# State products of a Mamba-2 mixer: C's high and low parts side by side, three matmuls made into two

## The chip, the cores and the metric

The kernel runs on one core of a Trainium2 chip. Its time is the device time of one launch in microseconds (us), the median of several runs; lower is better. The engines are named as in the profile: PE does matmuls (PEld is its weight load), DVE and ACT do elementwise work, POOL little here, and SP issues transfers. Each engine takes its instructions in the order of its own queue.

## What is computed

One decoder block over 512 tokens of width 1024, in float32: a token mixer, a cross-attention into 256 memory tokens and a SwiGLU feed-forward layer, each behind an RMSNorm. The mixer has a Mamba-2 part of 16 heads of width 64 in two groups, and a pooling part. The change lies in the Mamba-2 part, whose core is this (four chunks of 128 tokens, 128 states):

```python
cb = jnp.einsum("bclgn,bcsgn->bgcls", cc, bc)
y_diag = jnp.einsum("bghcls,bcsghp->bclghp", cb[:, :, None] * seg, xc)
states = jnp.einsum("bcsgn,bghcs,bcsghp->bcghpn", bc, decay_states, xc)
...
_, prev = lax.scan(step, init, (jnp.moveaxis(states, 1, 0), jnp.moveaxis(chunk_decay, -1, 0)))
y_off = jnp.einsum("bclgn,cbghpn,bghcl->bclghp", cc, prev, jnp.exp(a_cs))
```

`cc` is C, `bc` is B, `cb` the product of C with B in each chunk, and `y_off` what a chunk takes from the state left by the chunks before it.

## The kernel before

**Number format.** Every float32 operand of a matmul is split into a high part (a rounded copy, made by ACT) and a low part (the remainder, a subtraction on DVE). A product is three matmuls (`mm3`, L116 to L119): high by high, high by low, low by high, added up in PSUM. A name that ends in h or l is such a part, `whi` and `wlo` those of a weight. So `t_prh` and `t_prl` are the parts of a state, `t_cth` and `t_ctl` those of C.

**Slots.** The work is a table of slots (`SPEC`, L40 on). An item has up to three phases: prep ahead of its matmuls, its matmuls, and post behind them. The program is written slot by slot: post of the slot before and prep of the slot after, step by step in turn with the splitting of coming weights, then the slot's matmuls. A scheduler then makes the order of each engine's queue from this program by its own estimate of when operands are there, and gives out the buffers. Only the first slot keeps the written order.

**The items that matter here.**

- `cb:g` (L539): the product of C with B for group g, 12 matmuls of 128 columns into one PSUM bank. Its post multiplies by the causal mask on DVE (L552) into `t_cbm`.
- `s:g.c` (L586): the state left by chunk c, built up on DVE (L601, L603) as `t_prev`, then split (`t_prh` at L233 on ACT, `t_prl` at L241 on DVE).
- `P:j` (L624), one for each of eight pairs of heads (four pairs to a group). Its prep makes the decay matrix: eight relu on ACT (L645), exponentials (L651, L653), times `t_cbm` on DVE (L656), a high part `mh` on ACT (L660) and a low part `ml` on DVE (L663). Its matmuls are the state term `yo` (9 of 128 columns, three for each of chunks 1 to 3, which need the state left by chunks 0 to 2) and the diagonal product `pd` (12 of 256 columns). Its post makes `t_y` from `pd` (L687), multiplies `yo` by the decay E (L694) and adds it (L695).
- `v:m` and `p:g`: the pooling part's projection (24 matmuls of 512 columns) and its product `po` (12); post of `v` is a running sum on DVE (L749 to L754) and a split into `t_pdh`, `t_pdl`; post of `po` is a split into `t_pgh`, `t_pgl` (L235, L243). `z:m` is a gate's projection and `op:m` the pooling half of the output projection, 24 matmuls each.

The second group's part of the table is this; the place that the prediction speaks of is `P:4` and what lies around it:

```python
"v:4 t:1.2 s:1.0 g:3", "v:5 s:1.1", "p:1", "v:6 s:1.2", "P:4 v:7", "P:5 p:2", "z:7", "", "", "P:6 z:6 p:3",
"P:7", "op:0 g:5 op:1 op:2 g:6", ...
```

**Buffers.** PSUM has eight banks of 128x512 float32. Six of them are handed round to all products (`PS`, tag `ps`, L71); the other two are the single buffer of `pd`. A product's bank is free again when its post has read it.

Of the kernel before, what the change touches and what calls it, by code (L numbers as in the profile page):

```python
# [17 lines left out]
NC = 4  # L18
# [43 lines left out]
def hybrid_block(ctx: ExitStack, tc: tile.TileContext, a: dict, out: bass.AP,  # L62
                 act_bufs=69, la=1, wb=(6, 4, 5), eng="", dact=(0, 1), raw_n=6, warm=12, spec=None, start=START, smm=START_MM, hu=1, dbg=None):
    nc = tc.nc
# [27 lines left out]
    def col(i, rows=None):  # L92
        return vec[:, i:i + 1] if rows is None else vec[rows, i:i + 1]
# [22 lines left out]
    def mm3(ps, whi, wlo, xhi, xlo, start, stop):  # L116
        nc.tensor.matmul(ps, whi, xhi, start=start, stop=False)  # L117
        nc.tensor.matmul(ps, whi, xlo, start=False, stop=False)  # L118
        nc.tensor.matmul(ps, wlo, xhi, start=False, stop=stop)  # L119
# [103 lines left out]
    def need(*key):  # L223
        while key not in st:
            yield

    def splits(dsts, names, srcs, scale=None):

        out_ = []
        for (b, n), src in zip(names, srcs):  # L230
            hi = T(b + "h", F32R, n)
            if scale is None:
                nc.scalar.copy(hi, src)  # L233
            else:
                nc.scalar.activation(hi, src, AF.Identity, scale=scale)  # L235
            out_.append(hi)
        yield
        for key, (b, n), src, hi in zip(dsts, names, srcs, out_):
            lo = T(b + "l", F32R, n)
            if scale is None:  # L240
                nc.vector.tensor_tensor(out=lo, in0=src, in1=hi.bitcast(F32), op=ALU.subtract)  # L241
# [19 lines left out]
    st = {}  # L261
# [70 lines left out]
    def hold(it, name):  # L332
        it.ps = PS(name)
        return it.ps
# [157 lines left out]
    def i_xbc(i):  # L492
        m = XBC_ORDER[i]
        g = i // 6
        it = Item(keys=[("xbc", i)])

        def mm():
            proj(hold(it, "xbc"), ready[("xbc", i)], st["xg" if i < raw_n else "u"])

        def post():  # L500
            yield from need("r1")
            xr = mul("xr", it.ps, st["r1",]) if i < raw_n else it.ps
            y = T("cv")
            nc.scalar.activation(y, xr, AF.Identity, scale=col(V_CW + 3 * 12 + m), bias=col(V_CB + m))
            yield
            for s in (1, 2, 3):
                nc.vector.scalar_tensor_tensor(out=y[:, s:], in0=xr[:, :S - s],
                                               scalar=col(V_CW + (3 - s) * 12 + m),
                                               in1=y[:, s:], op0=ALU.mult, op1=ALU.add)
            nc.scalar.activation(y, y, AF.Silu)  # L510
            if i % 6 == 0:
                yield from splits([("B", g)], [("bt", 512)], [y])
                st["Bf", g] = y
            elif i % 6 == 1:
                yield from splits([("C", g)], [("ct", 512)], [y])
            else:
                st["xs", m] = y
            yield

        it.mm, it.post = mm, post  # L520
        return it


    def i_btm(g):
# [11 lines left out]
        it.mm, it.post = mm, post  # L536
        return it

    def i_cb(g):  # L539
        it = Item()  # L540

        def mm():
            bh, bl = st["B", g]
            ch, cl = st["C", g]
            ps = hold(it, "cb")
            for c in range(NC):
                cs = slice(c * P, (c + 1) * P)
                mm3(ps[:, cs], bh[:, cs], bl[:, cs], ch[:, cs], cl[:, cs], True, True)

        def post():  # L550
            t = T("cbm")
            nc.vector.tensor_tensor(out=t.rearrange("p (c l) -> p c l", l=P),  # L552
                                    in0=it.ps.rearrange("p (c l) -> p c l", l=P),
                                    in1=cmask.unsqueeze(1).broadcast_to([P, NC, P]), op=ALU.mult)
            st["cbm", g] = t

        it.mm, it.post = mm, post
        return it
# [65 lines left out]
    def i_pair(j, load=None):  # L624
        g, i = j // 4, j % 4
        it = Item()
        js = slice(i * P, (i + 1) * P)

        def prep():
            tok = st["tok"]  # L630
            if load is not None:
                load_abc(load)
            mh = act.tile([P, NC, 2, P], F32R, tag="m", name=nm("mh"), bufs=2)
            ml = act.tile([P, NC, 2, P], F32R, tag="m2", name=nm("ml"), bufs=2)
            E = st["E", j]
            Ds = []
            for q in range(2):
                h = 2 * j + q
                abc = st["abc", j][q]
                D = T("D")  # L640
                Ds.append(D)
                for c in range(NC):
                    cs = slice(c * P, (c + 1) * P)
                    if q in dact:
                        nc.scalar.activation(D[:, cs], abc[:, cs], AF.Relu, scale=-1.0,  # L645
                                             bias=tok[:, c, 32 + h:33 + h])
                    else:
                        nc.vector.tensor_scalar(out=D[:, cs], in0=abc[:, cs], scalar1=tok[:, c, 32 + h:33 + h],
                                                scalar2=0.0, op0=ALU.subtract, op1=ALU.min)
            yield  # L650
            nc.scalar.activation(E, E, AF.Exp)  # L651
            for q in range(2):
                nc.scalar.activation(Ds[q], Ds[q], AF.Exp, scale=-1.0 if q in dact else 1.0)  # L653
                yield
            for q in range(2):
                nc.vector.tensor_tensor(out=Ds[q], in0=Ds[q], in1=st["cbm", g], op=ALU.mult)  # L656
                yield
            Mv = [D.rearrange("p (c l) -> p c l", l=P) for D in Ds]
            for q in range(2):
                nc.scalar.copy(mh[:, :, q, :], Mv[q])  # L660
                yield
            for q in range(2):
                nc.vector.tensor_tensor(out=ml[:, :, q, :], in0=Mv[q], in1=mh.bitcast(F32)[:, :, q, :],  # L663
                                        op=ALU.subtract)
                yield
            it.mh, it.ml, it.E = mh, ml, E

        def mm():
            mh, ml = it.mh, it.ml
            ch, cl = st["C", g]  # L670
            it.po = PS("yo")
            for c in range(1, NC):
                ph, pl = st["pr", g, c]
                cs = slice(c * P, (c + 1) * P)
                mm3(it.po[:, (c - 1) * P:c * P], ph[:, js], pl[:, js], ch[:, cs], cl[:, cs], True, True)
            it.pd = psum.tile([P, 1024], F32, tag="pd", name=nm("pd"), bufs=1)
# [5 lines left out]
        def post():  # L682
            y = T("y")
            xs = st["xs", j]
            for q in range(2):
                rows = slice(64 * q, 64 * q + 64)
                nc.vector.scalar_tensor_tensor(  # L687
                    out=y[rows].rearrange("p (c l) -> p c l", l=P),
                    in0=xs[rows].rearrange("p (c l) -> p c l", l=P),
                    scalar=col(V_DSK + j, rows),  # L690
                    in1=it.pd[rows].rearrange("p (c q l) -> p c q l", q=2, l=P)[:, :, q, :],
                    op0=ALU.mult, op1=ALU.add)
                yield
            nc.vector.tensor_tensor(out=it.E, in0=it.po[:, 0:384], in1=it.E, op=ALU.mult)  # L694
# [801 lines left out]
```

## Time and profile before

| | |
|---|---|
| median of 3 runs | 795.74 us (794.84 to 796.38) |
| profiled execution | 796.13 us, of it span 794.4 us |
| PE busy | 782.7 us, 99% of the span |
| DVE busy | 632.9 us, 80% |
| ACT busy | 496.5 us, 63% |
| granted TensorE clock, mean | 0.996 |

The span runs from the first to the last instruction; 1.7 us of the execution lie around it. A row of a timeline gives the start in us from the span's start, the duration in us, engine, line, operation, and what is written from what. In a bracket stands how long the engine sat idle before and what released it. A row of groups gives the durations in ns (minimum, median, maximum), first and last start, and the shape. A row of windows gives for each engine the busy time of the window, then the granted clock, the share of the DMA engines and the rate in GB/s. Rows of the same kind on one engine overlap a little, so the price of one in a queue is the distance of two starts.

### The profile page before, as it was taken

The page shows a single profiled execution, that of the slowest core. Times are in us where ns is not written, and L with a number is a line of the kernel's source. Part 1 is how long each engine was busy: PE and PEld are TensorE (multiplying, and loading weights), DVE is VectorE, ACT ScalarE, POOL GpSimd, SP SyncE. Part 2 cuts the span into 40 slices and gives each one's busy share as a digit, 9 for nine tenths or more (in the row PEclk, how much of TensorE's full clock was granted, in tenths as well). Part 3 has the DMA queues.
Part 4 walks back from the last instruction along what each step waited for, and adds up shares of the span by engine and source line. Part 5 has one row for each costly group of instructions (what it writes and reads, how often), then busy time and mean ns, then how long its engine had stood idle before and what let it go on. Part 6 is the DMA issues. An engine that isn't in the chain of part 4 may idle for free.

```text
span 794.4 us, 10540 instructions
## 1 busy us (share of the span) xinstructions
PE 782.7 (99%) x3844; PEld 659.0 (83%) x3844; DVE 632.9 (80%) x937; ACT 496.5 (63%) x791; POOL 49.8 (6%) x66
## 2 busy tenths in 40 slices
PE   9999999999999999999999999999999999999995
PEld 7878888888888889888888888888888888888984
DVE  7999969999895799675766667888866788867897
ACT  8668699657953547455655695665455665455845
POOL 0000000000000000000000011011101011101000
PEclk9999999999999999999999999999999999999998
DMA  8253335124475235765355268797779797869602
GB/s 331 90 172 106 114 92 179 54 100 132 153 261 162 97 106 149 170 176 171 132 131 142 72 135 228 176 263 148 247 159 282 179 245 164 248 156 269 163 14 106
DMA packets 41283, 128.62 MB, mean 162 GB/s; under 512 B 4864, under 2 KB 7296, under 8 KB 41232
## 3 DMA queue, kind: packets, MB, share of 16 engines
q1 hardware_dynamic: 33024, 99.30, 36.8%
q0 software_dynamic: 8064, 28.58, 19.8%
q8 instruction: 30, 0.49, 0.2%
q14 instruction: 21, 0.17, 0.1%
q10 hardware_dynamic: 144, 0.07, 0.0%
HBM read 116.63 MB, written 2.13 MB: 149 GB/s over the span
## 4 chain that ended last, share of the span: by engine, by line
PE 86%; DVE 8%; ACT 2%; DMA 1%; issue 1%; SPq 0%; DVEq 0%
PE gA L1087 15%; PE gB L1087 8%; PE dA L1087 5%; PE gC L1087 4%; PE dB L1087 2%; PE vAB L1087 2%; DVE wlo L205 2%; PE wo L117 2%; PE wo L119 2%; PE op L119 2%; PE op L117 2%; PE op L118 2%; PE q L117 2%; PE os L117 2%; PE q L118 2%; PE os L119 2%
## 5 line engine op out<-in xcount | busy, mean ns | idle before, releaser
L203 ACT CAST whi<-raw 128x1024 fp32r<-128x1024 f32 (+1 forms) x125 | 129.0, 1040 | 96.0 <-issue 14.2
L205 DVE TENSOR_TENSOR wlo<-raw,whi 128x1024 fp32r<-128x1024 f32 (+1 forms) x125 | 149.9, 1208 | 32.0 <-ACT whi L203 30.9
L203 ACT CAST whi<-wq 128x1024 fp32r<-128x1024 f32 (+1 forms) x76 | 77.4, 1028 | 76.2 <-PE gA L1087 19.3
L205 DVE TENSOR_TENSOR wlo<-wq,whi 128x1024 fp32r<-128x1024 f32 (+1 forms) x76 | 90.2, 1193 | 39.8 <-ACT whi L203 39.6
L172 POOL DMA_DIRECT2D raw<-w_s x38 | 32.7, 863 | 644.4 <-DVE t_vx L868 311.5
L1087 PE MATMUL gA<-whi,t_xh 128*128 128x512 f32 (+1 forms) x192 | 71.7, 373 | 0.0
L1087 PE MATMUL gA<-wlo,t_xh 128*128 128x512 f32 (+1 forms) x192 | 71.4, 372 | 0.0
L1087 PE MATMUL gA<-whi,t_xl 128*128 128x512 f32 (+1 forms) x192 | 71.3, 371 | 0.0
L1087 PEld LDWEIGHTS gA<-wlo,t_xh 128*128 128x128 f32 x192 | 36.2, 188 | 6.3
L1087 PEld LDWEIGHTS gA<-whi,t_xl 128*128 128x128 f32 x192 | 36.2, 188 | 6.2
L1087 PEld LDWEIGHTS gA<-whi,t_xh 128*128 128x128 f32 x192 | 36.2, 188 | 6.2
L1103 ACT ACTIVATE t_gu<-t_gu,s 128x512 f32<-128x512 f32 (+1 forms) x24 | 16.4, 688 | 31.7 <-DVE t_gu L1099 31.7
L1087 PE MATMUL dA<-whi,t_xh 128*128 128x512 f32 x88 | 34.1, 392 | 0.4 <-DVE t_hT L1244 0.2
L1087 PE MATMUL dA<-whi,t_xl 128*128 128x512 f32 x88 | 34.2, 389 | 0.0
L1087 PE MATMUL dA<-wlo,t_xh 128*128 128x512 f32 x88 | 34.1, 390 | 0.0
L194 DVE TENSOR_TENSOR wq<-wq,wq 128x1024 f32<-128x1024 f32 (+1 forms) x19 | 22.5, 1193 | 13.5 <-DMA wq<-raw 13.4
L1087 PE MATMUL gB<-whi,t_xq 128*128 128x512 f32 (+1 forms) x96 | 27.5, 371 | 0.0
L117 PE MATMUL z<-t_uh,whi 128*128 128x512 f32 x64 | 25.2, 394 | 0.4 <-ACT t_uh L233 0.4
L1165 ACT CAST t_xh<-t_x 128x512 fp32r<-128x512 f32 x30 | 18.6, 621 | 10.5 <-DVE t_x L1184 6.4
L117 PE MATMUL wo<-t_oh,whi 128*128 128x512 f32 x64 | 25.2, 394 | 0.0
L117 PE MATMUL v<-t_uh,whi 128*128 128x512 f32 x64 | 25.1, 392 | 0.0
L117 PE MATMUL q<-t_hgh,whi 128*128 128x512 f32 x64 | 25.1, 392 | 0.0
(401 smaller groups left out, 2242.5 us busy)
## 6 DMA issues: line engine op xcount, KB each, us to landing
raw<-w_u SPq DMA_DIRECT2D x68, 512.0 KB, 3.4
raw<-w_s SPq DMA_DIRECT2D x54, 512.0 KB, 4.4
wq<-w_s SPq DMA_DIRECT2D x36, 512.0 KB, 5.4
raw<-w_s POOLq DMA_DIRECT2D x36, 512.0 KB, 7.3
wq<-raw POOLq DMA_DIRECT2D x17, 512.0 KB, 7.8
t_x<-xT SPq DMA_DIRECT2D x16, 256.0 KB, 5.6
t_abc<-d_acs SPq DMA_DIRECT2D x16, 256.0 KB, 4.4
out<-t_hT SPq DMA_DIRECT2D x8, 256.0 KB, 2.3
```

What stands on the lines that cost most here:

```text
L117: nc.tensor.matmul(ps, whi, xhi, start=start, stop=False)
L118: nc.tensor.matmul(ps, whi, xlo, start=False, stop=False)
L119: nc.tensor.matmul(ps, wlo, xhi, start=False, stop=stop)
L172: nc.gpsimd.dma_start(sw[c, f][:, :n], quad("11" if f == 7 else "22"), accum_op=ALU.add)
L194: add = nc.vector.tensor_tensor(out=sw[c, 3][:, :n], in0=sw[c, 3][:, :n], in1=sw[c, 6][:, :n], op=ALU.add)
L203: nc.scalar.copy(hi[:, :n], raw[:, :n])
L205: nc.vector.tensor_tensor(out=lo[:, :n], in0=raw[:, :n], in1=hi.bitcast(F32)[:, :n], op=ALU.subtract)
L1087: nc.tensor.matmul(it.ps[tt], p[:, ts_], w[:, ws], start=first, stop=(c, i, n) == pairs[-1] and p is xh and w is wl, skip_group_check=True)
L1103: st["silu"] = nc.scalar.activation(g, g, AF.Silu, scale=st["r3",][:, c:c + 1])
L1165: nc.scalar.copy(h if w is None else h[:, w], src)
```

## The change

C's two parts are kept side by side: two tiles hold two chunks each, 128 columns of the high part beside 128 of the low part for every chunk. One matmul of 256 columns then multiplies a high weight by both, and one of 128 columns adds the low weight by the high part to the first half (`mm2`). The two halves of the result have to be added afterwards: ACT copies the low half out of PSUM and DVE adds the high half to it. A chunk's result takes 256 columns of PSUM in place of 128, so `cb` and `yo` take two banks each.

```diff
@@ i_xbc, post
-                yield from splits([("C", g)], [("ct", 512)], [y])
+                c2 = [T("ct", F32R) for _ in range(2)]
+                v = [t.rearrange("p (c q l) -> p c q l", q=2, l=P) for t in c2]
+                w = y.rearrange("p (b c l) -> p b c l", b=2, l=P)
+                for b in range(2):
+                    nc.scalar.copy(v[b][:, :, 0, :], w[:, b])
+                yield
+                for b in range(2):
+                    nc.vector.tensor_tensor(out=v[b][:, :, 1, :], in0=w[:, b], in1=v[b].bitcast(F32)[:, :, 0, :],
+                                            op=ALU.subtract)
+                st["C", g] = [c2[c // 2][:, 256 * (c % 2):256 * (c % 2) + 256] for c in range(NC)]
@@
+    def mm2(ps, whi, wlo, x, start=True):
+
+        n = x.shape[-1] // 2
+        nc.tensor.matmul(ps, whi, x, start=True, stop=False, skip_group_check=True)
+        nc.tensor.matmul(ps[:, 0:n], wlo, x[:, 0:n], start=False, stop=True, skip_group_check=True)
+
@@ i_cb, mm and post
-            ch, cl = st["C", g]
-            ps = hold(it, "cb")
+            it.ps = [PS("cb") for _ in range(2)]
             for c in range(NC):
                 cs = slice(c * P, (c + 1) * P)
-                mm3(ps[:, cs], bh[:, cs], bl[:, cs], ch[:, cs], cl[:, cs], True, True)
+                mm2(it.ps[c // 2][:, 256 * (c % 2):256 * (c % 2) + 256], bh[:, cs], bl[:, cs], st["C", g][c])
...
+            for b in range(2):
+                nc.scalar.copy(tv[:, b], pv[b][:, :, 1, :])
+            yield
+            for b in range(2):
+                nc.vector.tensor_tensor(out=tv[:, b], in0=pv[b][:, :, 0, :], in1=tv[:, b], op=ALU.add)
@@ i_pair, mm
-            ch, cl = st["C", g]
-            it.po = PS("yo")
+            it.po = [PS("yo") for _ in range(2)]
             for c in range(1, NC):
                 ph, pl = st["pr", g, c]
-                cs = slice(c * P, (c + 1) * P)
-                mm3(it.po[:, (c - 1) * P:c * P], ph[:, js], pl[:, js], ch[:, cs], cl[:, cs], True, True)
+                o = 256 * ((c - 1) % 2)
+                mm2(it.po[(c - 1) // 2][:, o:o + 256], ph[:, js], pl[:, js], st["C", g][c])
@@ i_pair, post
+            yo = T("yo", n=384)
...
+            for d, _, low in parts:
+                nc.scalar.copy(d, low)
...
-            nc.vector.tensor_tensor(out=it.E, in0=it.po[:, 0:384], in1=it.E, op=ALU.mult)
+            for d, high, _ in parts:
+                nc.vector.tensor_tensor(out=d, in0=high, in1=d, op=ALU.add)
+            nc.vector.tensor_tensor(out=it.E, in0=yo, in1=it.E, op=ALU.mult)
```

Line numbers grow with it: the new matmuls are L551 and L552, the adds of a pair L722, its copies L709, and a line of a pair's prep or post moves by 21 to 29.

The scheduler makes a new order from the new program. Three places of it follow, each before and now. The first is PE at pair 4. The numbers behind a name count tiles, so they differ between the two; `t_prh_374` and `t_prl_376` before, `t_prh_384` and `t_prl_386` now are the second state of the group, `t_prh_410` and `t_prl_412` before, `t_prh_420` and `t_prl_422` now the third. Before:

```order
L117 MATMUL yo_414_1917<-t_cth_163_832,t_prh_374_1769 128x128
L118 MATMUL yo_414_1917<-t_ctl_169_849,t_prh_374_1769 128x128
L117 MATMUL v_416_1940<-t_uh_72_354,whi_389_1815 128x512
L119 MATMUL yo_414_1917<-t_cth_163_832,t_prl_376_1774 128x128
L118 MATMUL v_416_1940<-t_ul_82_384,whi_389_1815 128x512
L119 MATMUL v_416_1940<-t_uh_72_354,wlo_390_1816 128x512
L117 MATMUL v_416_1940<-t_uh_73_356,whi_389_1815 128x512
```

Now:

```order
L551 MATMUL yo_424_1935<-t_ct_164_835,t_prh_384_1787 128x256
L552 MATMUL yo_424_1935<-t_ct_164_835,t_prl_386_1792 128x128
L117 MATMUL pd_426_1943<-mh_394_1819,t_xch_328_1573 128x256
...
L119 MATMUL pd_426_1943<-mh_394_1819,t_xcl_337_1596 128x256
L551 MATMUL yo_425_1936<-t_ct_164_835,t_prh_420_1917 128x256
L117 MATMUL v_427_1956<-t_uh_73_356,whi_399_1833 128x512
L118 MATMUL v_427_1956<-t_ul_82_386,whi_399_1833 128x512
L119 MATMUL v_427_1956<-t_uh_73_356,wlo_400_1834 128x512
```

The pair's twelve `pd` matmuls and the first one of its second `yo` bank (`yo_425`, which reads the third state) moved from behind `v` to ahead of it.

The second is ACT after pair 4's `mh`, where pair 5's relu (`t_D_404`, `t_D_405` before, `t_D_414`, `t_D_415` now) and the third state's high part stand. Before:

```order
L660 CAST mh_384_1801<-t_D_387_1808 128x4x128
L203 CAST whi_463_2198<-raw_388_1813 128x1024
L645 ACTIVATE t_D_404_1878<-t_abc_381_1794,tok_799 128x128 x4
L645 ACTIVATE t_D_405_1883<-t_abc_382_1796,tok_799 128x128 x4
L233 CAST t_prh_410_1899<-t_prev_398_1866 128x512
L653 ACTIVATE t_D_404_1878<-t_D_404_1878 128x512
```

Now:

```order
L681 CAST mh_394_1819<-t_D_397_1826 128x4x128
L666 ACTIVATE t_D_414_1896<-t_abc_391_1812,tok_801 128x128 x4
L666 ACTIVATE t_D_415_1901<-t_abc_392_1814,tok_801 128x128 x4
L674 ACTIVATE t_D_414_1896<-t_D_414_1896 128x512
L674 ACTIVATE t_D_415_1901<-t_D_415_1901 128x512
L233 CAST t_prh_420_1917<-t_prev_408_1884 128x512
```

The weight cast went elsewhere, and both exponentials of pair 5 (L653, now L674) moved ahead of the third state's high part.

The third is PE at pairs 6 and 7 (pair 6 is `pd_452` before and `pd_467` now, pair 7 is `pd_498` now). Before, at the start of pair 6's `pd`:

```order
L117 MATMUL op_497_2298<-t_pgh_392_1823,whi_463_2198 128x512
L117 MATMUL pd_452_2131<-mh_440_2073,t_xch_318_1557 128x256
L118 MATMUL op_497_2298<-t_pgl_393_1826,whi_463_2198 128x512
L119 MATMUL op_497_2298<-t_pgh_392_1823,wlo_464_2199 128x512
L117 MATMUL op_497_2298<-t_pgh_431_2028,whi_463_2198 128x512
L118 MATMUL pd_452_2131<-ml_441_2074,t_xch_318_1557 128x256
```

Now, at its end:

```order
L119 MATMUL pd_467_2153<-mh_454_2097,t_xcl_337_1596 128x256
L551 MATMUL yo_497_2266<-t_ct_164_835,t_prh_420_1917 128x256
L552 MATMUL yo_497_2266<-t_ct_164_835,t_prl_422_1924 128x128
L117 MATMUL pd_498_2273<-mh_461_2124,t_xch_328_1573 128x256
L118 MATMUL pd_498_2273<-ml_462_2125,t_xch_328_1573 128x256
```

Matmuls of `op` stood among and behind pair 6's `pd`; now they stand behind pair 7's.

More of the change, by code (lines that the diff above doesn't have):

```diff
@@ L543, in mm @@
             bh, bl = st["B", g]
-            ch, cl = st["C", g]
-            ps = hold(it, "cb")
+            it.ps = [PS("cb") for _ in range(2)]
             for c in range(NC):
                 cs = slice(c * P, (c + 1) * P)
-                mm3(ps[:, cs], bh[:, cs], bl[:, cs], ch[:, cs], cl[:, cs], True, True)
+                mm2(it.ps[c // 2][:, 256 * (c % 2):256 * (c % 2) + 256], bh[:, cs], bl[:, cs], st["C", g][c])
         def post():
             t = T("cbm")
+            tv = t.rearrange("p (b c l) -> p b c l", b=2, l=P)
+            pv = [ps.rearrange("p (c q l) -> p c q l", q=2, l=P) for ps in it.ps]
+            for b in range(2):
[3 more added lines that the diff above has]
+                nc.vector.tensor_tensor(out=tv[:, b], in0=pv[b][:, :, 0, :], in1=tv[:, b], op=ALU.add)
             nc.vector.tensor_tensor(out=t.rearrange("p (c l) -> p c l", l=P),
-                                    in0=it.ps.rearrange("p (c l) -> p c l", l=P),
+                                    in0=t.rearrange("p (c l) -> p c l", l=P),
                                     in1=cmask.unsqueeze(1).broadcast_to([P, NC, P]), op=ALU.mult)
@@ L682, in post @@
         def post():
+            yo = T("yo", n=384)
+            parts = [(yo[:, 0:256].rearrange("p (c l) -> p c l", l=P),
+                      it.po[0].rearrange("p (c q l) -> p c q l", q=2, l=P)),
+                     (yo[:, 256:384], it.po[1][:, 0:256].rearrange("p (q l) -> p q l", l=P))]
+            parts = [(d, v[..., 0, :], v[..., 1, :]) for d, v in parts]
+            for d, _, low in parts:
+                nc.scalar.copy(d, low)
             y = T("y")
```

## Prediction

> **What bounds the kernel now.** I read the busy shares and the chain of waits on the page, then the waits of PE, then the timelines of the engines around the place that the waits point to.
>
> ```profile
> span 794.4 us, 10540 instructions
> PE 782.7 (99%) x3844; PEld 659.0 (83%) x3844; DVE 632.9 (80%) x937; ACT 496.5 (63%) x791; POOL 49.8 (6%) x66
> PE 86%; DVE 8%; ACT 2%; DMA 1%; issue 1%; SPq 0%; DVEq 0%
> ```
>
> PE is busy for 782.7 of 794.4 us, and 86% of the chain that ended last is PE. Taken alone, this says that every matmul saved is time saved. But 8% of the chain is DVE, so there is a stretch in which PE runs at DVE's pace. The list of PE's waits (us in total, times, longest) has one inside the run that is as long as this:
>
> ```profile
> PE yo L119 <- DVE t_prl L241: 0.4, 1, 0.4
> ```
>
> It is the state term `yo` waiting for the low half of a state. The chain (first two rows) and PE's timeline place it at pair 4:
>
> ```profile
> 178.81 0.61 DVE t_prl L241
> 179.46 0.33 PE yo L119
> ...
> 178.60 0.45 PE L117 MATMUL v<-t_uh,whi 128*128 128x512 f32 x1
> 184.94 0.22 PE L117 MATMUL yo<-t_cth,t_prh 128*128 128x128 f32 x1
> 187.46 0.28 PE L117 MATMUL pd<-mh,t_xch 128*128 128x256 f32 x1
> 189.46 0.28 PE L119 MATMUL pd<-mh,t_xcl 128*128 128x256 f32 x1
> 191.42 0.22 PE L117 MATMUL yo<-t_cth,t_prh 128*128 128x128 f32 x1
> ```
>
> PE loses only 0.4 us there because ready work stands right behind the late operand: 24 matmuls of `v` up to 184.94, then `yo` of pair 5 and the pool products `po`, before the pair's own `pd` at 187.46 and the third state's columns (c=3) at 191.42. The windows show whose pace it is (columns PE, PEld, DVE, ACT busy us):
>
> ```profile
> 140.00:150.00 10.00, 10.00 (x62) 8.88 (x62) 8.71 (x14) 6.39 (x11) 0.00 (x0) 1.00 0.32 107
> 150.00:160.00 10.00, 10.00 (x46) 8.28 (x45) 9.94 (x20) 5.49 (x9) 0.00 (x0) 1.00 0.00 0
> 160.00:170.00 10.00, 10.00 (x48) 8.27 (x47) 9.90 (x16) 5.36 (x8) 0.00 (x0) 1.00 0.30 105
> 170.00:180.00 10.00, 9.59 (x46) 7.83 (x45) 10.00 (x19) 5.96 (x11) 0.00 (x0) 1.00 0.41 131
> 180.00:190.00 10.00, 10.00 (x54) 8.57 (x53) 8.82 (x15) 10.00 (x27) 0.00 (x0) 1.00 0.57 183
> ```
>
> From 150 to 180 DVE has 0.16 us of 30 free, and from 180 to 190 ACT is full. What the change adds to DVE ahead of 180 delays the state by nearly as much.
>
> **What the change saves on PE.** A group of three matmuls becomes one of 256 columns and one of 128. Neighbouring starts give the price:
>
> ```profile
> 113.93 0.27 PE L117 MATMUL yo<-t_cth,t_prh 128*128 128x128 f32 x1
> 114.26 0.27 PE L117 MATMUL yo<-t_cth,t_prh 128*128 128x128 f32 x1
> 115.00 0.28 PE L117 MATMUL pd<-mh,t_xch 128*128 128x256 f32 x1
> 115.36 0.28 PE L117 MATMUL pd<-mh,t_xch 128*128 128x256 f32 x1
> ```
>
> Three of 128 take 0.33 us (114.26 - 113.93), 0.11 each; three of 256 take 0.36, 0.12 each. The new group takes 0.12 + 0.11 = 0.23, so 0.105 is saved. There are 32 groups (8 of `cb`, 24 of `yo`): 3.35 us. Of it 0.84 (`cb`) and the four early pairs' 1.26 fall before 179, 1.26 after. The 2.1 us before 179 do not reach the end: PE comes earlier to products whose inputs DVE makes, and from 146 on DVE is the later one.
>
> **What it adds on DVE and ACT.**
>
> ```profile
> L694 DVE TENSOR_TENSOR t_E<-yo,t_E x8: 548/557/559, 114.8 to 211.3; 128x384 f32<-128x384 f32 x8
> L324 DVE TENSOR_TENSOR t_macc<-t_macc,t_sq x7: 418/425/426, 240.4 to 256.3; 128x256 f32<-128x256 f32 x7
> L323 ACT ACTIVATE t_sq<-t_mem x7: 402/409/419, 240.0 to 255.0; 128x256 f32<-128x256 f32 x7
> ```
>
> An add of 128x256 is taken at 0.425 us, which in a queue is some 0.08 less (512 columns, rows below: 0.68 long, and the next starts 0.60 later). So a pair adds 0.35 + 0.22 = 0.57 on DVE, and two copies of about 0.5 together on ACT; a `cb` adds two of each. No row shows an add that reads alternate 128 column pieces of PSUM; the 128x384 row, which reads PSUM, is on the same line of price per column (0.557), so I take no extra. The bounds are 0 (hidden in a gap) and the full 0.77 unpipelined a pair. The added work of `cb` and of C's split lies before 146, where DVE has gaps (8.71 of 10 us busy from 140 to 150), and I cost it at nothing; without that cover it would be about 1.7 us.
>
> In the busy stretch the scheduler's new order puts 2.4 us more ahead of the second state's low half: pair 3's adds (0.57), one more weight split `wlo` moved ahead (1.14), one more accumulation of squares (0.60). The prices of the last two are start to start (175.02 to 176.15, 176.15 to 176.75):
>
> ```profile
> 175.02 1.21 DVE L205 TENSOR_TENSOR wlo<-raw,whi 128x1024 fp32r<-128x1024 f32 x1
> 176.15 0.68 DVE L603 TENSOR_TENSOR t_prev<-t_prev,st 128x512 f32<-128x512 f32 x1
> 176.75 1.26 DVE L750 TENSOR_TENSOR_SCAN t_vs<-t_v,t_vs 128x504 f32<-128x504 f32 x1
> 178.72 0.69 DVE L241 TENSOR_TENSOR t_prl<-t_prev,t_prh 128x512 fp32r<-128x512 f32 x1
> 186.02 0.69 DVE L663 TENSOR_TENSOR ml<-t_D,mh 128x512 fp32r<-128x512 f32 x1
> ```
>
> That state, ready at 179.41 before, is ready at about 181.9.
>
> **What now stands behind the late state.** This is the term that decides. A pair's `yo` takes two of the six banks in place of one. The second (c=3 alone) is given out ahead of `v`'s, and in the new order on PE its first matmul stands ahead of `v`. That matmul reads the high half of the third state. So the queue reads: `yo` c=1, c=2 (second state), twelve `pd` (need `ml`), `yo` c=3 (needs `prh` of the third state), and only then the 24 ready matmuls of `v`. No cover is left: PE waits three times in a row. The times follow from ACT's rows of before, moved by what is ahead of them:
>
> ```profile
> 178.84 0.62 ACT L233 CAST t_pdh<-t_vd 128x512 fp32r<-128x512 f32 x1 [0.40 <-DVE t_vd L753]
> 179.94 2.45 ACT L645 ACTIVATE t_D<-t_abc,tok 128x128 f32<-128x128 f32 x8
> 182.29 0.63 ACT L653 ACTIVATE t_D<-t_D 128x512 f32<-128x512 f32 x1
> 185.31 0.62 ACT L660 CAST mh<-t_D 128x512 fp32r<-128x512 f32 x1
> 185.82 1.07 ACT L203 CAST whi<-raw 128x1024 fp32r<-128x1024 f32 x1
> 186.77 2.47 ACT L645 ACTIVATE t_D<-t_abc,tok 128x128 f32<-128x128 f32 x8
> 189.13 0.62 ACT L233 CAST t_prh<-t_prev 128x512 fp32r<-128x512 f32 x1
> ```
>
> ACT's first t_D group starts 2.5 later (182.45, behind t_pdh and one t_pgh), so `ml` ends at 186.71 + 2.5 = 189.2 and `pd` runs from 189.2 to 190.6. On ACT the second `mh` ends at 188.5. Here the weight cast of 185.82 is no longer ahead (-0.95), but both exponentials of pair 5 are (+1.05): eight relu (2.36, from 186.77 to 189.13) to 190.9, two exponentials to 192.0, `prh` to 192.6. So `v` starts at about 192.65, and ends with 24 x 0.229 us and one `yo` at 198.25, where before it ended at 184.94.
>
> The sum: +13.3 for `v`'s end; -1.43 for pair 4's `pd`, which is done by then, and -0.34 for its c=3; -0.95 for the shorter `yo` of pairs 5 to 7. That is +10.6.
>
> **A second, smaller stall.** `pd` has one buffer. Before, matmuls of `op` stood between pair 6's `pd` and pair 7's; now all twelve of pair 7 stand right behind pair 6's, with `op` after them. PE must wait for both y's of pair 6, with two `ml` between them on DVE:
>
> ```profile
> L687 DVE SCALAR_TENSOR_TENSOR t_y<-t_cv,vec,pd x16: 728/745/756, 117.5 to 224.9; 64x512 f32<-64x512 f32 x16
> ```
>
> 0.7 + 0.6 + 0.6 + 0.75 = 2.6, less 0.2 for two `yo` matmuls between: +2.4 (0 if DVE had been let past; 2.6 at most). After that the two orders agree, PE is back to back, and nothing is won back.
>
> The whole is +13.0. The profiled execution takes 796.13 us with 1.7 around its span, 0.4 above the median of 795.74, so it goes to about 809.1 and the median to 808.7.
>
> Bounds: if `prh` came at before's own 189.75, `v` would start 2.9 earlier; without the second stall 2.4 less; if DVE's stretch began 2.1 us earlier with PE's saving, 2.1 less: +5.6, 801.3. Above: 1.7 if the early DVE work is not hidden, and 0.2 a pair if the adds are not pipelined: +15.5, 811.2.
>
> **The clock.** PE would stand idle from 181.9 to 189.2. After its last matmul of this run, which ends at 786.06, the granted clock (the column that reads 1.00, then 0.65) falls:
>
> ```profile
> 786.00:787.00 1.00, 0.06 (x1) 0.00 (x0) 1.00 (x4) 0.82 (x3) 0.00 (x0) 1.00 0.00 0
> 788.00:789.00 1.00, 0.00 (x0) 0.00 (x0) 0.86 (x3) 0.97 (x4) 0.00 (x0) 0.65 1.03 391
> ```
>
> 0.65 in that microsecond, if it ends at half, puts the fall at 788.3, 2.2 us after the end. So `pd` at 189.2 would start at half clock and take 2.86 in place of 1.43: to 192.06, still before 192.6, so it costs nothing. How long the clock takes to rise again no row shows; if as long as the fall, it is up before `v`. I take 0, with 5.5 (all of `v` at half) as the far end. [...]
>
> **Rivals.**
> *PE's work decides after all.* The saving of 3.35 counts in full: 792.4. For it speaks that PE is 99% busy. It needs the third state's `prh` cast when PE gets there, at 178 to 179: some 13 us earlier than the walk gives and 11 earlier than before's own 189.75. The scheduler placed the matmul there, which only says that its estimate found it ready.
> *Only the shift.* PE waits for the second state 2.4 us longer, but other ready work covers the rest: +2.4 -0.95 = +1.5, 797.2. That needs work ahead of c=3 that the order does not have, or `prh` at 182.
> *The clock costs in full.* PE stays at half for the first 2.2 us or more of `v`, and again behind the second stall: +2 to +5.5 on top, about 811.
>
> **Chances.** The stall as worked out 0.68 (801 to 811); with the clock on top 0.14; only the shift 0.10; PE's work 0.08. The predicted time is 808.7. The range 799 to 813 leaves out PE's case and most of the shift's. About 0.2% (1.6 us) is what a measurement can tell from no change: faster 0.08, within 0.05 (half of the shift's), slower 0.87.
>
> **What would show it.** In the changed profile, PE's waits should hold a wait of the first `yo` lines for `t_prl` or DVE, one of `pd` for `ml`, about 7 us, and one of c=3 for ACT's `t_prh`, about 2; the window from 180 to 190 should have PE under 3 of 10. `pd` of pair 7 should wait about 2.4 for t_y. Starts of a new group should be 0.23 apart. After about 230 the two runs should be a constant distance apart. The prediction is wrong if PE is back to back through 180 to 190, or if the distance grows elsewhere: at `cb` near 95 to 135, or in `op`.

## The result and the profile after

The changed kernel takes 817.80 us (median of 4 runs, 816.15 to 818.38) against 795.66 for the kernel before: ratio 1.0274, 95% interval 1.0262 to 1.0287. It is slower, as forecast, but by 22.1 us where 13.0 were forecast, and outside the range of 799 to 813.

The page of the changed kernel (span, busy shares, chain by engine):

```profile
span 816.7 us, 10522 instructions
PE 787.8 (96%) x3812; PEld 660.1 (81%) x3812; DVE 639.5 (78%) x959; ACT 501.5 (61%) x813; POOL 49.9 (6%) x66
PE 78%; DVE 12%; ACT 5%; issue 2%; DMA 2%; SPq 0%; DVEq 0%; ACTq 0%
```

PE's share of the chain fell from 86% to 78%, and DVE and ACT took it up. PE's busy time rose by 5.1 us although it issues 32 matmuls fewer: the same matmuls took longer somewhere. DVE's rose by 6.6, ACT's by 5.0, with the copies and adds. The list of PE's waits (us in total, times, longest), which had the state's 0.4 us and another 0.4 us of a `z` at 54 us inside the run, now has these:

```profile
PE pd L117 <- ACT mh L681: 6.3, 2, 6.0
PE yo L551 <- ACT t_z L738: 4.3, 1, 4.3
PE yo L552 <- DVE t_prl L241: 2.1, 1, 2.1
PE yo L551 <- ACT t_prh L233: 1.4, 2, 0.9
...
PE pd L117 <- DVE t_y L714: 1.0, 1, 1.0
```

PE's timeline at pair 4, with the waits that were forecast one behind the other:

```profile
182.85 0.47 PE L552 MATMUL yo<-t_ct,t_prl 128*128 128x128 f32 x1 [2.12 <-DVE t_prl L241]
189.35 0.58 PE L117 MATMUL pd<-mh,t_xch 128*128 128x256 f32 x1 [6.03 <-ACT mh L681]
190.13 0.58 PE L118 MATMUL pd<-ml,t_xch 128*128 128x256 f32 x1 [0.20 <-DVE ml L684]
...
193.71 0.58 PE L551 MATMUL yo<-t_ct,t_prh 128*128 128x256 f32 x1 [0.87 <-ACT t_prh L233]
194.09 0.63 PE L117 MATMUL v<-t_uh,whi 128*128 128x512 f32 x1
194.52 0.63 PE L118 MATMUL v<-t_ul,whi 128*128 128x512 f32 x1
...
200.03 0.39 PE L117 MATMUL v<-t_uh,whi 128*128 128x512 f32 x1
200.26 0.40 PE L118 MATMUL v<-t_ul,whi 128*128 128x512 f32 x1
...
228.46 0.58 PE L551 MATMUL yo<-t_ct,t_prh 128*128 128x256 f32 x1 [4.28 <-ACT t_z L738]
```

The first matmuls of `v` start 0.43 us apart, later ones 0.23: PE works at half clock for a while after the stall (a granted clock of 0.50 up to 199.24, by the finer windows further below). The last row is a second stall, at pair 7. The windows show both (PE, PEld, DVE, ACT busy us, then the granted clock):

```profile
170.00:180.00 10.00, 9.77 (x45) 7.99 (x43) 10.00 (x17) 6.31 (x10) 0.00 (x0) 1.00 0.20 61
180.00:190.00 10.00, 1.44 (x3) 0.76 (x3) 7.83 (x15) 7.86 (x20) 0.00 (x0) 0.61 0.71 221
190.00:200.00 10.00, 9.00 (x28) 7.46 (x29) 8.35 (x16) 6.23 (x16) 0.00 (x0) 0.54 0.06 21
...
220.00:230.00 10.00, 5.38 (x30) 4.53 (x29) 7.65 (x14) 9.97 (x23) 0.00 (x0) 0.83 0.48 159
```

Where the time went is read most directly by the start of the same matmul in the two timelines (the first of a product, or a fixed one of its row; all in us from the span's start):

```
                               before   changed   distance
first po (p:0)                 153.80   153.18     -0.62
v:6, first matmul              171.98   173.31     +1.33
z:7, first matmul              189.82   206.97    +17.15
po of p:3, first matmul        203.88   218.59    +14.71
op, 49th matmul                221.46   243.33    +21.87
mixer's norm (ry)              254.10   275.97    +21.87
```

So: 0.6 us saved up to 153, 2.0 lost by 172, 13.4 net at pair 4 (17.15 at its worst; some 2.4 come back because pair 4's pd and chunk 3, and shorter state terms, are done or cheaper by then), 7.2 at pairs 6 and 7, and next to nothing after.

### The profile page after: what moved, and what is told of

It is laid out like the page before. It is cut to its first block, busy times and chain, and to the rows that moved or that the text cites. A ratio compares the mean times of both kernels' runs of the same rounds, so it can differ in the third digit from the quotient of the medians.

```text
span 816.7 us, 10522 instructions
## 1 busy us (share of the span) xinstructions
PE 787.8 (96%) x3812; PEld 660.1 (81%) x3812; DVE 639.5 (78%) x959; ACT 501.5 (61%) x813; POOL 49.9 (6%) x66
## 4 chain that ended last, share of the span: by engine, by line
PE 78%; DVE 12%; ACT 5%; issue 2%; DMA 2%; SPq 0%; DVEq 0%; ACTq 0%
PE gA L1116 15%; PE gB L1116 7%; PE dA L1116 5%; PE gC L1116 4%; PE dB L1116 2%; DVE wlo L205 2%; PE vAB L1116 2%; PE op L117 2%; PE op L118 2%; PE op L119 2%; PE wo L119 2%; PE wo L117 2%; PE q L117 2%; PE os L118 2%; PE q L118 2%
## 5 line engine op out<-in xcount | busy, mean ns | idle before, releaser
L118 PE MATMUL v<-t_ul,whi 128*128 128x512 f32 x64 | 26.0, 406 | 0.0
L119 PE MATMUL v<-t_uh,wlo 128*128 128x512 f32 x64 | 25.9, 404 | 0.0
L117 PE MATMUL op<-t_pgh,whi 128*128 128x512 f32 x64 | 25.4, 396 | 0.0
```

## Experiments

Theory: the second PSUM bank of a pair's state term takes the bank that let ready matmuls stand ahead of late ones, so PE meets three late operands in a row; the rest follows from the low clock behind the stall and from a like stall at pairs 6 and 7. Rival: the copies and adds on ACT and DVE are what costs, whatever order PE has.

**The bank without the work, and the work without the bank.** `e1_banks_only` is the kernel before with two banks for `yo`:

```diff
-            it.po = PS("yo")
+            it.po = [PS("yo") for _ in range(2)]
...
-                mm3(it.po[:, (c - 1) * P:c * P], ph[:, js], pl[:, js], ch[:, cs], cl[:, cs], True, True)
+                o = P * ((c - 1) % 2)
+                mm3(it.po[(c - 1) // 2][:, o:o + P], ph[:, js], pl[:, js], ch[:, cs], cl[:, cs], True, True)
...
-            nc.vector.tensor_tensor(out=it.E, in0=it.po[:, 0:384], in1=it.E, op=ALU.mult)
+            for b, n in ((0, 256), (1, 128)):
+                Eb = it.E[:, 256 * b:256 * b + n]
+                nc.vector.tensor_tensor(out=Eb, in0=it.po[b][:, 0:n], in1=Eb, op=ALU.mult)
```

> The kernel before with one edit: the state term of a pair gets two PSUM banks in place of one (chunks 1 and 2 in one, chunk 3 in the other), all matmuls as before, no copies and no adds; only the multiply by E is cut in two (256 and 128 columns). Theory 'bank' (the second bank puts chunk 3's matmul, which reads the late third state, ahead of v in PE's queue): PE stalls again between 180 and 190 with nothing else changed; DVE lacks the added 2.4 us, so the stall is some 2 us shorter than in the changed kernel: 806 to 812 us. Rival 'added work' (the copies and adds on ACT and DVE are what costs): within 2 us of before, 794 to 798.

Measured: 810.40 us, ratio 1.0188 (1.0173 to 1.0203). PE's timeline of this run, at pair 4:

```profile
179.70 0.33 PE L119 MATMUL yo<-t_cth,t_prl 128*128 128x128 f32 x1 [0.76 <-DVE t_prl L241]
186.22 0.58 PE L117 MATMUL pd<-mh,t_xch 128*128 128x256 f32 x1 [6.19 <-ACT mh L660]
186.99 0.58 PE L118 MATMUL pd<-ml,t_xch 128*128 128x256 f32 x1 [0.19 <-DVE ml L663]
190.59 0.48 PE L117 MATMUL yo<-t_cth,t_prh 128*128 128x128 f32 x1 [0.88 <-ACT t_prh L233]
```

The same waits, with no matmul, copy or add changed, and about 3 us earlier than in the changed kernel. The first `z:7` matmul starts 13.84 us later than before.

`e2_adds_only` is the kernel before with copies and DVE instructions of the changed kernel's size:

```diff
+            yo = T("yo", n=384)
+            parts = [(yo[:, 0:256], it.po[:, 0:256]), (yo[:, 256:384], it.po[:, 256:384])]
+            for d, s in parts:
+                nc.scalar.copy(d, s)
...
-            nc.vector.tensor_tensor(out=it.E, in0=it.po[:, 0:384], in1=it.E, op=ALU.mult)
+            for d, s in parts:
+                nc.vector.tensor_tensor(out=d, in0=s, in1=d, op=ALU.max)
+            nc.vector.tensor_tensor(out=it.E, in0=yo, in1=it.E, op=ALU.mult)
```

> The kernel before with the added work alone: nine matmuls into one bank as before, then ACT copies 256 and 128 columns of it out and DVE combines them with the bank in two instructions of the changed kernel's size (a maximum of the value with its own copy, so the value stays). Theory 'bank': PE's order at pair 4 stays as before, with v behind the late state, so the 0.57 us a pair on DVE move the second state's low half by 1 to 3 us and nine matmuls of v (2 us) cover most of it: 795.5 to 799. Rival 'added work': most of the 22 us is here, over 805.

Measured: 804.86 us, ratio 1.0114 (1.0097 to 1.0131). That is neither forecast, and close to the rival's: the work alone costs 9.2 us. The distances say where: +1.09 at `v:6`, +3.33 at `z:7`, +4.33 at p:3's `po`, +8.95 at `op`. So pair 4 costs some 2 us here, not 13, and the larger part is at pair 7, where PE waits for a bank that ACT empties:

```profile
PE op L117 <- ACT t_z L715: 2.8, 1, 2.8
```

Behind that wait PE works at about half its pace from 221.40 to 224.66 (starts of `pd` 0.21 apart in place of 0.12, of `op` 0.43 in place of 0.23), which by an estimate from these starts costs another 1.5 us; the two make up most of the 4.6 us by which the distance grows there. Each cause alone is dear, and they act in different places: the bank mostly at pair 4, the work mostly at pair 7. The rival was half right.

**Which edit of the change.** `e3_yo_only` puts `cb` back, `e4_cb_only` puts the state term back (C stays side by side in both):

```diff
-                mm2(it.ps[c // 2][:, 256 * (c % 2):256 * (c % 2) + 256], bh[:, cs], bl[:, cs], st["C", g][c])
+                cc = st["C", g][c]
+                mm3(ps[:, cs], bh[:, cs], bl[:, cs], cc[:, 0:P], cc[:, P:2 * P], True, True)
...
```

> The changed kernel with the product of C with B back in three matmuls, one bank and no adds; C side by side and the state term as changed. Both theories put the loss into the state term: 815 to 819. If cb's part matters (its two banks, or its adds before 146 us), this is more than 1.5 us off the changed kernel.

Measured: 816.90 us, ratio 1.0267 (1.0251 to 1.0282): the state term is all of it but about 1 us.

```diff
-                mm2(it.po[(c - 1) // 2][:, o:o + 256], ph[:, js], pl[:, js], st["C", g][c])
+                mm3(it.po[:, (c - 1) * P:c * P], ph[:, js], pl[:, js], cc[:, 0:P], cc[:, P:2 * P], True, True)
...
```

> The changed kernel with the state term back in three matmuls, one bank and no adds; C side by side and cb as changed. Both theories: the order around pair 4 is that of before, and cb's saving of 0.84 us on PE either reaches the end (794.9) or is eaten where PE waits for DVE (795.7): 794.5 to 796.5. Over 797 would say that cb's adds delay DVE's busy stretch.

Measured: 795.67 us, ratio 0.9995 (0.9986 to 1.0004): no difference. The profiled run is 0.44 us ahead from `z:7` on, about half of the 0.84 that `cb` saves, and that is too little for the comparison to tell.

**Is it pair 4's bank, or too few banks in general?** `e9_bank_pair4` is `e1_banks_only` with `range(2 if j in (4,) else 1)`.

> The kernel before with the second bank for pair 4 alone (its chunk 3 in a bank of its own, E's multiply cut in two there); the other seven pairs, all matmuls and all DVE and ACT work as before. PE's order again has pair 4's pd and chunk 3 ahead of v. Theory 'bank at pair 4': nearly all of what the second bank cost for all pairs (14.7 us) is here: 806 to 811. Rival 'banks short everywhere' (each pair's second bank costs a part): 797 to 803.

Measured: 810.30 us, ratio 1.0181 (1.0167 to 1.0195), against 810.40 with the bank in all eight pairs. One bank, at one place, costs what all cost. The wait before its `pd` is 6.18 us, that of chunk 3's matmul 0.88, as in `e1_banks_only`. So a shortage spread over the stage is ruled out: what decides is the second bank at pair 4. The cut of E's multiply, which comes with the bank here, is hardly the cause: `e12_one_bank` below cuts it in two in every pair and has no stall at pair 4. Why the scheduler's estimate puts `pd` and chunk 3 ahead of `v` once there are two banks, no run shows.

**What the clock costs.** `e5_filled` keeps PE busy through the stall with products that are overwritten:

```diff
+            def fill(ps, n):
+                for _ in range(n if j in (4,) else 0):
+                    nc.tensor.matmul(ps[:, 0:256], st["pr", g, 2][0][:, js], st["C", g][2], start=True, stop=True,
+                                     skip_group_check=True)
...
+                if c == 3:
+                    fill(it.pd, 82)
```

> The changed kernel with 82 extra matmuls of 256 columns (0.12 us each at full clock) into pair 4's pd buffer ahead of its pd, which overwrites them: 17 in the wait for the second state's low half, 65 in the wait for the decay matrix. Orders of all engines are otherwise those of the changed kernel, and the fillers end before chunk 3's operand is there. Theory 'clock': PE stays warm through the stall, the first 12 matmuls of v take 0.228 in place of 0.427 us, the stall at pair 4 costs 2.4 us less, and the second stall keeps its own: 814.5 to 816.5. Rival 'waits only' (the low granted clock costs nothing that the waits do not already cost): 817 to 818.5.

Measured: 817.03 us (814.94 to 817.97), ratio 1.0264 (1.0250 to 1.0278); against the changed kernel's 817.80 no clear difference, and the time lies in the rival's range. Yet the mechanism shows in the timeline of the profiled run:

```profile
195.29 0.39 PE L551 MATMUL yo<-t_ct,t_prh 128*128 128x256 f32 x1 [1.77 <-ACT t_prh L233]
195.52 0.39 PE L117 MATMUL v<-t_uh,whi 128*128 128x512 f32 x1
195.75 0.39 PE L118 MATMUL v<-t_ul,whi 128*128 128x512 f32 x1
```

`v` runs at 0.23 a matmul from its first one. It starts 1.43 us later than in the changed kernel, but its 13th matmul comes 0.95 earlier: 2.38 us gained over twelve matmuls, as expected. The late start is not one of the clock: in this run ACT waited for a transfer ahead of the second `mh`,

```profile
190.13 0.53 ACT L672 ACTIVATE t_E<-t_E 128x384 f32<-128x384 f32 x1 [1.46 <-DMA t_E<-d_acs]
```

so the price of the clock at pair 4 is shown in this trace, and the total of this run is not a clean measure of it.

**Covering the stalls again.** `e6_v_first` exchanges `"P:4 v:7"` for `"v:7 P:4"` in the slot table.

> The changed kernel with one word of the slot table exchanged: v:7 ahead of P:4 in their slot. PE's new order has all 24 matmuls of v (5.5 us) ahead of pair 4's yo; pd and chunk 3 still follow directly. Theory 'bank and order': v fills the wait for the second state and part of that for the decay matrix, v is then not behind the third state, so 5.5 us of the stall and most of the half clock after it go; the second stall at pairs 6 and 7 stays: 806 to 812. Rival 'added work' (DVE and ACT are late whatever PE does meanwhile): over 815.

Measured: 816.06 us, ratio 1.0252 (1.0236 to 1.0267): 1.7 us gained where 6 to 12 were expected, and the time lies in the rival's range. `v` does run inside the stall, but its 5.5 us do not cover it, and the operands come later still: the second `mh` at 190.01 (189.30 in the changed kernel), behind a wait of 0.54 us of ACT for a transfer, and the third state's high part at 195.23 (193.66), behind a weight cast that moved back ahead of it:

```profile
PE pd L117 <- ACT mh L681: 5.4, 2, 4.6
PE yo L551 <- ACT t_z L738: 4.3, 1, 4.3
PE yo L551 <- ACT t_prh L233: 1.8, 1, 1.8
```

PE still stands for 4.6 and 1.8 us, and the matmuls after that still run at about half the pace (`pd` 0.21 apart, `po` 0.43). Before the change there stood between the second state's product and the pair's `pd` not only `v` but pair 5's `yo` and most of `po`, some 8 us. At p:3's `po` the run is 4.2 us ahead of the changed kernel; part of that is given back at pair 7, whose wait is as long as before (3.0 ahead at `op`).

`e10_op_first` aims at pair 7 alone: `op:0` gets a slot of its own ahead of `P:7`.

```diff
-    "P:7", "op:0 g:5 op:1 op:2 g:6", "op:6 g:4 op:3 g:7",
+    "op:0", "P:7", "g:5 op:1 op:2 g:6", "op:6 g:4 op:3 g:7",
```

> The changed kernel with op:0 in a slot of its own ahead of P:7, so that 18 matmuls of op stand between pair 6's pd and pair 7's yo. Theory: the second stall is PE waiting for ACT's second t_z (a bank) with nothing between; 15 op matmuls (3.4 us) then fill most of its 4.3 us, and the half clock after it (2.4 us) goes: 811.5 to 814. Rival: ACT and DVE set the end of this stretch anyway, and op waits later for t_pgl: 816 to 818.

Measured: 812.05 us, ratio 1.0202 (1.0188 to 1.0216), 5.8 us less than the changed kernel, and as expected. The wait for t_z is gone from PE's list, and from p:3's `po` to `op` the distance to the kernel before grows from 15.17 to 15.92, in place of 14.71 to 21.87. So the second stall is worth some 6.4 of its 7.2 us and is one of order, too: nothing stood there to be done.

`e7_table_new` re-cuts the table for both places, `e8_table_old` is the same table with the kernel before:

```diff
-    "P:4 v:7", "P:5 p:2", "z:7", "", "", "P:6 z:6 p:3",
-    "P:7", "op:0 g:5 op:1 op:2 g:6",
+    "v:7 p:2", "z:7 P:4", "P:5", "", "z:6", "P:6 p:3",
+    "op:0", "P:7", "g:5 op:1 op:2 g:6",
```

> The changed kernel with the slot table re-cut around pairs 4 to 7: v:7 and p:2 in the slot ahead, z:7 ahead of P:4, z:6 in an empty slot, op:0 ahead of P:7. PE's order then has v, twelve po and 24 z (13.7 us of ready work) between the third state's product and pair 4's yo, and 18 op ahead of pair 6's pd. Theory 'bank and order': with cover back, the 14.7 and 7.2 us are gone and what is left is PE's saving against what DVE delays: 793 to 798. Rival 'added work': 802 or more, with PE waiting for DVE or ACT at several places.

> The same table with the kernel before (three matmuls, one bank, no adds). It is what e7 is to be held against: 794 to 797, since PE was 99% busy already. If e7 is 1 to 3 us below it, the shorter state term is worth its 3.35 us of PE once its waits are covered; if e7 is above it, the added work costs more than the saving even then.

Measured: 806.44 us for the changed form (1.0136, 1.0122 to 1.0149) and 799.93 for the old one (1.0059, 1.0046 to 1.0072). With 13.7 us of ready work ahead of pair 4 the long waits there are gone, and 11.4 us of the changed kernel's time with them. But two new ones stand in PE's list, which the old form does not have:

```profile
PE z L117 <- DVE t_pgl L243: 3.1, 1, 3.1
PE yo L551 <- DVE t_pgl L243: 3.0, 1, 3.0
```

`t_pgl` is DVE's read of a pool product out of its bank. Neither matmul reads it, so PE waits there for no operand but, as the profile has it, for a free bank. At the same table the changed form is 6.5 us slower than the old one. Both expectations were too low: the changed form came out in the rival's range, with the waits for DVE that the rival named. Moving the cover costs something by itself, 4.3 us with the old form, and the trace of that run shows where:

```profile
202.14 0.48 PE L117 MATMUL pd<-mh,t_xch 128*128 128x256 f32 x1 [2.35 <-DVE t_y L687]
```

Behind it PE works at about half its pace from 202.41 to 205.62 (`pd` 0.21 apart, `z` 0.43), by the same kind of estimate some 1.5 us more. That is the profiled run, which at 801.61 us is the longest of the five.

**Can a part of it pay?** `e11_early_only` uses the new form for `cb` and pairs 0 to 3, the old one for pairs 4 to 7.

```diff
+            it.old = j in (4, 5, 6, 7)
+            it.po = [PS("yo") for _ in range(1 if it.old else 2)]
...
+                if it.old:
+                    mm3(it.po[0][:, (c - 1) * P:c * P], ph[:, js], pl[:, js], cc[:, 0:P], cc[:, P:2 * P], True, True)
```

> The changed form for cb and for pairs 0 to 3 (32 - 12 = 20 of 32 groups, 2.1 us of PE), the old form (three matmuls, one bank, no adds) for pairs 4 to 7. PE's order from 170 us on is that of before. Theory 'DVE eats it': 2.1 us are saved by 150 us and lost again where PE waits for DVE at 160 to 180: 794.8 to 796.8. Rival 'PE decides': 793.3 to 794.3.

Measured: 799.87 us, ratio 1.0055 (1.0041 to 1.0069): slower, which neither case had. With the old form from pair 4 on there is no stall, but PE is 0.42 ahead at 154, not 2.1, and 1.53 behind at `v:6`:

```profile
131.36 0.36 PE L117 MATMUL pd<-mh,t_xch 128*128 128x256 f32 x1 [1.04 <-DVE t_y L719]
160.72 0.50 PE L118 MATMUL po<-t_pdl,whi 128*128 128x512 f32 x1 [0.61 <-DVE t_pdl L241]
164.53 0.50 PE L117 MATMUL v<-t_uh,whi 128*128 128x512 f32 x1 [0.78 <-ACT t_v L780]
```

All three are waits for DVE or ACT. The last, for `t_v`, stands in `e2_adds_only` too (0.77 at 164) and not in `e1_banks_only`, which speaks for the early pairs' copies and adds as its cause; for the other two that is not shown.

`e12_one_bank` computes only chunk 1 in the new form, so that a pair's 512 columns fit one bank:

```diff
+                if c == 1:
+                    mm2(it.po[:, 0:256], ph[:, js], pl[:, js], cc)
+                else:
+                    mm3(it.po[:, c * P:(c + 1) * P], ph[:, js], pl[:, js], cc[:, 0:P], cc[:, P:2 * P], True, True)
```

> C side by side, cb in three matmuls; of a pair's yo only chunk 1 in the changed form (256 and 128 columns), chunks 2 and 3 in three matmuls each, so that all 512 columns fit one bank. One copy (ACT) and one add (DVE) of 128 columns a pair, and E's multiply cut in two. Saves 0.84 us of PE in all. Theory 'bank': no stall at pair 4, PE's order stays near that of before, and DVE's 0.3 us a pair cost about as much as is saved: 795 to 799. Rival 'added work' (the 9.2 us that copies and adds cost in the one bank form come mostly from their number, not their size): 802 to 806.

Measured: 803.72 us, ratio 1.0095 (1.0081 to 1.0109), inside the rival's range. There is no stall at pair 4 (+1.31 at `z:7`), but between p:3's `po` and `op` the distance goes from 3.05 to 7.35, as in `e2_adds_only`. PE's list names t_y, with pair 7's `pd`:

```profile
PE pd L117 <- DVE t_y L706: 1.7, 2, 1.5
...
PE pd L118 <- DVE ml L678: 0.9, 1, 0.9
```

Behind these two waits at pair 7 (1.46 and 0.88 us) PE works at about half its pace from 220.07 to 223.28 (`pd` 0.22 apart, `op` 0.43), by the same kind of estimate another 1.5 us. A third of the columns of extra work (128 of 384 a pair) cost 7.9 us, nearly as much as all of them in `e2_adds_only`. So the cost does not follow the length of ACT's and DVE's extra instructions; that their place in the order decides is the likely reading, and which of them it is at pair 7 was not tried one by one. None of the versions beats the kernel before.

## Why the prediction was wrong

The direction, the place and the mechanism at pair 4 were right; the range was not, mainly because of two terms of the sum.

- *What bounds the kernel now; the saving on PE.* Right. Pair 5's three groups start at 202.10 and its `pd` at 202.74, 0.21 a group where 0.23 was worked out. That the 2.1 us before 179 do not reach the end was right in direction and too kind: up to 153 only 0.6 was kept (a wait of 1.05 us of pair 3's `pd` for t_y, at 131), and by `v:6` it had turned to 1.33 lost.
- *The added work at `cb` and C, costed at nothing.* Right: `e4_cb_only` shows no difference.
- *DVE 2.4 us later at the second state.* Too small by 0.9. The three terms add up to 2.3; the state's low half, forecast for 181.9, was there at 182.79, 3.4 later than before, in the wait of 2.12 shown above. The delay goes with the added work: in `e2_adds_only`, which has that work and one bank, the low half is there at 182.68, in `e1_banks_only`, which has the banks alone, at 179.64. What the forecast missed is that DVE's stretch was no longer full. From 150 to 180 DVE stood idle for 1.35 us, where it was 0.16 before, most of it in two waits for ACT, which `e2_adds_only` has too:

```profile
163.31 1.22 DVE L205 TENSOR_TENSOR wlo<-raw,whi 128x1024 fp32r<-128x1024 f32 x1 [0.44 <-ACT whi L203]
...
168.60 0.69 DVE L241 TENSOR_TENSOR t_pdl<-t_vd,t_pdh 128x512 fp32r<-128x512 f32 x1 [0.69 <-ACT t_pdh L233]
```

- *The three waits in a row.* Right in their order, and shown to be the bank's doing by `e1_banks_only` and `e9_bank_pair4`. `v` was forecast for 192.65 and came at 194.09: the walk along ACT's queue held to about 1.4 us, of which 0.9 was DVE's. That `pd`'s first matmul came at 189.35, with 189.2 forecast, is chance: the forecast was for `ml`, which was there at 190.08, and the matmul at 189.35 waited for `mh` alone. The third wait, forecast at about 2, was 0.87, because `pd` ran longer at half clock.
- *The clock, taken at 0.* This is the first step that failed. I had the fall nearly right (it was to come during the wait for `ml`, and came at 182.17, in the wait for `t_prl` ahead of it) and assumed that the clock rises as fast as it falls, 2.2 us. The granted clock in finer windows of the changed kernel (the first row is part full and part half, the last part half and part full):

```profile
182.00:182.50 0.50, 0.00 (x0) 0.00 (x0) 0.50 (x2) 0.28 (x1) 0.00 (x0) 0.67 0.07 8
...
183.00:186.00 3.00, 0.32 (x1) 0.14 (x1) 1.23 (x2) 3.00 (x10) 0.00 (x0) 0.50 0.99 302
...
192.00:195.00 3.00, 2.13 (x8) 1.64 (x8) 2.56 (x7) 2.95 (x6) 0.00 (x0) 0.50 0.00 0
...
199.00:199.50 0.50, 0.50 (x3) 0.36 (x3) 0.00 (x0) 0.00 (x0) 0.00 (x0) 0.76 0.00 0
```

It stayed at half through pair 4's `pd` and twelve matmuls of `v`, which took 0.427 in place of 0.228 each: 2.4 us, the 2.38 that `e5_filled` got back. A rival had it (0.14, "+2 to +5.5 on top"); it came in both stalls. Its 811 was still too low, because it kept the small second stall.
- *The second, smaller stall, 2.4, 2.6 at most.* This is the second step that failed. Place and mechanism were right in part, the size was not: 4.28 of waiting, then 2.3 at half clock (twelve `pd` 2.67 in place of 1.43, five `op` 1.98 in place of 1.14, two `yo` 0.25 more), and smaller waits around them; 7.2 us in all. I priced the two `ml` between the y's by their length alone. But ACT was full (9.97 of 10 us from 220 to 230), and DVE stood waiting for it (2.01 us). ACT's timeline of the changed kernel:

```profile
226.51 1.28 ACT L738 ACT_TABLE_LOAD   x1
227.81 0.60 ACT L738 ACTIVATE t_z<-z 128x512 f32<-128x512 f32 x1
```

and DVE's:

```profile
224.55 1.29 DVE L677 TENSOR_TENSOR t_D<-t_D,t_cbm 128x512 f32<-128x512 f32 x2 [2.01 <-ACT t_D L674]
225.76 0.73 DVE L714 SCALAR_TENSOR_TENSOR t_y<-t_cv,vec,pd 64x512 f32<-64x512 f32 x1
226.42 1.28 DVE L684 TENSOR_TENSOR ml<-t_D,mh 128x512 fp32r<-128x512 f32 x2
227.73 0.76 DVE L714 SCALAR_TENSOR_TENSOR t_y<-t_cv,vec,pd 64x512 f32<-64x512 f32 x1
```

t_z frees the bank that pair 7's chunk 3 was given, at 228.41; the second y frees `pd` at 228.49. The forecast named only the second of these waits. ACT's queue sets both.
- *Nothing won back after that.* Right: the distance is +21.87 from `op` on.

In sum the forecast of 13.0 lacked 3.9 at pair 4 (1.4 later, 2.4 of clock) and about 5 at pair 7 (1.9 of waiting, 2.3 of clock, some 0.8 of smaller waits): 8.9, which is the difference to 21.9. The range failed because its upper end added up bounds for DVE's work and left out the clock and the waits for ACT.

## What to carry to other kernels

A form that saves matmuls but takes one more PSUM bank can cost far more than it saves (22.1 us here, where 3.35 of PE was to be saved), where the order that comes out of it leaves no ready work to run while a late operand is awaited: look at what stands behind each late operand in the new order, not at how much each engine has to do. When a forecast contains a stall of some microseconds on PE, price the half clock after it as part of the stall (2.4 and 2.3 us for the two stalls here). When an engine waits for two others, walk the full queue of the busiest of them up to the operand; the durations of the instructions between were a lower bound only here (2.4 worked out from them at pair 7, 4.28 waited).

## What the runs showed of the hardware

Two things that I had not expected.

- When the granted clock changed. The rows of the finer windows above put the fall of the changed kernel at 182.17 and the rise at 199.24, if each is part full and part half; these two do the same for the second stall:

```profile
226.50:227.00 0.50, 0.00 (x0) 0.00 (x0) 0.50 (x1) 0.48 (x1) 0.00 (x0) 0.54 1.10 434
233.00:233.50 0.50, 0.50 (x3) 0.40 (x2) 0.50 (x2) 0.50 (x2) 0.00 (x0) 0.63 0.88 262
```

That is a fall at 226.54 and a rise at 233.37. The four points are 17.07, 27.30 and 6.83 us apart, which is 5, 8 and 2 times 3.41. In these runs the clock neither fell nor rose a fixed time after PE stopped or began. In the changed kernel both falls came 2.4 us after dense work ended (179.8 and 224.2), the first although a single matmul ran in between (180.34), and the rises 5.5 and 4.9 us after work began again without a gap (193.71 and 228.46). In `e5_filled` dense work ended at 223.2, and the first matmul at half pace stands at 228.19, 5.0 us later and 0.7 us after PE had resumed (227.48). In `e1_banks_only` the windows read 0.56 from 180 to 190 and 0.76 from 190 to 200, which is 13.6 us at half, if the rest is full. And in the profiled run of `e8_table_old` a wait of 2.35 us was followed by 3.2 us of matmuls at half pace (202.41 to 205.62). What sets these times no run shows.
- One bank for one pair of eight is worth 14.4 us of 796 (`e9_bank_pair4`), and 128 columns of copy and add a pair, with E's multiply cut in two, cost about 8 (`e12_one_bank`), though over the run DVE was free for 20% of the time and ACT for 37%.
